# The down projection of a hybrid trunk: from a plain product to Strassen's seven, on one Trainium2 core

## The chip, the cores and the metric

The kernel runs on one core of one Trainium2 chip. The core has a matrix engine (PE, TensorE, with its weight loads listed as PEld), a vector engine (DVE, VectorE), a scalar engine (ACT, ScalarE), a general engine (POOL, GpSimd), and SyncE (SP), which here issues nearly all DMAs. Operands lie in SBUF (128 partitions), matmuls write PSUM. The metric is the device time of one execution in microseconds; less is better.

## The reference

One layer of a token mixer (an S5 state-space branch and an mLSTM branch) followed by a channel mixer, on 16 meta tokens and 2048 tokens of width 1024, in float32. The change is in the channel mixer:

```python
FFN_DIM = 2816

def channel_mixer(x, g_pre, g_post, w_gate, w_up, w_conv, b_conv, w_down):
    h = rmsnorm(x, g_pre)
    a = causal_dwconv(h @ w_gate, w_conv, b_conv)
    y = (jax.nn.gelu(a, approximate=True) * (h @ w_up)) @ w_down
    return x + rmsnorm(y, g_post)
```

The last product is the down projection: 2048 tokens x 2816 by 2816 x 1024. The result is normalised over its 1024 columns, scaled by `g_post` and added to x (in the kernel: to `h1_d`, the residual stream in DRAM).

## The kernel before

**Precision.** Every large product is made of three matmuls. An operand `a` is split into a high part (ScalarE copies `a` into the matmul type float32r) and a low part (VectorE subtracts the high part from `a`); `mm3` (lines 172 to 174) and `mm3x` (177 to 179) then add high x high, high x low and low x high into one PSUM tile. So each operand costs one ScalarE and one VectorE pass before TensorE may use it.

**The FFN stage.** `ffn_unit(p, m, ...)` handles block m (of NF = 22 blocks of 128 FFN channels) for token half p. Gate and up projections together are already one Strassen product: seven products of four depth blocks each, in the order 1, 6, 2, 7, 5, 4, 3, whose moving operands `op[n]` (sums of parts of the normalised input) stay in SBUF for the whole half, in pairs of tiles t4(0) to t4(11) and q4(0), q4(1). Each unit loads its weight blocks (`weights_first`, `weights_second`), forms the sums and splits them (`weight_op`, lines 1124 and 1125). For p = 0 a product runs in two pieces of 258 and 256 columns, for p = 1 in one of 512. After each product VectorE or ScalarE takes the PSUM tile into a running sum; then come the three-tap convolution (line 1254 on ScalarE, 1256 on VectorE), the GELU (1257), the product with the up projection (1261) and the store of the unit's y block to DRAM (`y_d`, line 1262, on SP's queue).

**Other work beside it.** In units 1 to 8 of p = 0 rows of the last token blocks are normalised (`norm_rows`, `norm_cols`); in units 10 to 17 `sums_piece` forms the sums that p = 1 needs as operands. In the last unit of p = 0, `turn` loads and splits four operands of p = 1 as their tiles come free. Staging tiles come from the pool `mk` (three places of about 1 MB).

**The down projection before.** It runs over two halves `nh` of 512 output columns. All 22 weight blocks of the half are loaded (four at a time through `mk`) and split (lines 1328 and 1329) into the tiles t4(0) to t4(10). Then for each of 16 tiles of 128 tokens the y blocks come back from DRAM in three chunks of 8, 8 and 6 (`ys`, line 1335), are split (1338, 1339) and serve as stationary operands of 22 x 3 matmuls of 512 columns into one PSUM tile. ScalarE forms the sum of squares (1345), VectorE multiplies by the gains. For `nh` = 0 the result stays in SBUF (`o0`); for `nh` = 1 the tile's row scale is computed (`rstd_of`, POOL at line 107), a row tile of `h1_d` is loaded, two multiply-adds (1358) make the output and two DMAs store it.

**What sets the order.** The tile framework keeps the program order of the code as a priority and orders each engine's instructions by a planned timeline; it adds all waits. On the chip each engine runs that order, one after the other, and each waits in place. Tiles of a pool take places as the tags are first used; a pool that is opened after another was closed lies where that one lay, and a new tile waits for the old tiles that it covers.

## Time and profile before

| | us |
|---|---|
| median of 3 runs | 2792.69 (2790.66 to 2794.34) |
| the profiled execution, its own time | 2792.36 |
| its span | 2790.6 |
| granted TensorE clock, mean | 0.998 |
| PE busy | 2759.1 |
| DVE busy | 1761.1 |
| ACT busy | 1054.7 |
| bytes moved by DMA | 395.47 MB, mean 142 GB/s |

The span is the time from the first to the last instruction of one profiled execution; times in a trace count from its start. A table by stretches gives, for each stretch of the span, the busy time of each engine with its instructions in brackets, then the granted clock (1.00 is full), the share of the 16 DMA engines that was busy, and GB/s. A row of a group gives line, engine, operation, output<-input, shape and count, then busy time in us and the mean of one in ns, then the idle time before it and what ended it. Matmuls are pipelined: the mean of one in such a row is longer than the distance to the next, so the rate is read from counts by time. The FFN stage lies between about 1430 and 2302 us, the down projection from 2287 to the end.

### The profile page before, as it was taken

To read this page: it belongs to the slowest core of one execution; us is meant where nothing else is said; L and a number is where in the kernel's file an instruction comes from. 1 tells how busy PE (TensorE), PEld (TensorE's weight loads), DVE (VectorE), ACT (ScalarE), POOL (GpSimd) and SP (SyncE) were. 2 spreads that over 40 slices of the span, in tenths; PEclk is the share of its full clock that TensorE was granted. 3 is DMA by queue.
4 is the path that set the end of the run, shared out by engine and by line. 5 is a ranking of instruction groups with operands and counts; after the bars stand their busy time and mean duration, and the time that the engine had idled before them with its cause. 6 is when DMAs were issued, how large, how long until landed. Compare 5 with 4: busy or idle time off the path is not lost.

```text
span 2790.6 us, 40815 instructions
## 1 busy us (share of the span) xinstructions
PE 2759.1 (99%) x15590; PEld 2484.9 (89%) x15590; DVE 1761.1 (63%) x3429; ACT 1054.7 (38%) x1979; POOL 136.8 (5%) x225
## 2 busy tenths in 40 slices
PE   8999999999999999999999999999999999999999
PEld 8999999999999987777799999998788788888887
DVE  4637799377555464676798887786776683224333
ACT  6102344233444444344354434453443352224221
POOL 1000000000000000000100000000000000000000
PEclk9999999999999999999999999999999999999999
DMA  9333443212454574667744462252222244335453
GB/s 309 106 79 131 158 147 121 71 69 72 145 159 144 167 212 121 223 196 250 265 157 138 159 234 87 73 176 85 80 80 81 79 145 149 99 90 165 157 166 128
DMA packets 323478, 395.47 MB, mean 142 GB/s; under 512 B 40321, under 2 KB 229142, under 8 KB 322642
## 3 DMA queue, kind: packets, MB, share of 16 engines
q1 hardware_dynamic: 323282, 392.86, 43.9%
q8 instruction: 122, 2.00, 0.3%
q14 instruction: 74, 0.61, 0.1%
HBM read 284.47 MB, written 108.31 MB: 141 GB/s over the span
## 4 chain that ended last, share of the span: by engine, by line
PE 82%; DMA 7%; DVE 6%; ACT 1%; issue 1%; POOL 1%; SPq 0%; DVEq 0%; POOLq 0%; ACTq 0%
PE mm L172 10%; PE mm L174 10%; PE mm L173 10%; PE ac L173 9%; PE ac L174 9%; PE ac L172 8%; PE ac L179 4%; PE ac L178 4%; PE ac L177 4%; PE mm L177 3%; PE mm L179 3%; PE mm L178 3%; DMA wu<-in_w_up_dram 2%; DMA gat<-gab_d 1%; DVE w L1125 1%
## 5 line engine op out<-in xcount | busy, mean ns | idle before, releaser
L174 PE MATMUL mm<-hTh,wl 128*128 128x410 f32 (+3 forms) x1216 | 428.0, 352 | 0.0
L172 PE MATMUL mm<-hTh,wh 128*128 128x410 f32 (+3 forms) x1216 | 427.6, 352 | 0.0
L173 PE MATMUL mm<-hTl,wh 128*128 128x410 f32 (+3 forms) x1216 | 427.4, 352 | 0.0
L1339 DVE TENSOR_TENSOR yhl<-ys,yhl 128x1024 fp32r<-128x1024 f32 (+1 forms) x96 | 109.1, 1137 | 291.9 <-ACT yhl L1338 291.9
L173 PE MATMUL ac<-t,yhl 128*128 128x512 f32 x704 | 278.5, 396 | 0.0
L174 PE MATMUL ac<-t,yhl 128*128 128x512 f32 x704 | 277.3, 394 | 0.0
L172 PE MATMUL ac<-t,yhl 128*128 128x512 f32 x704 | 276.6, 393 | 0.0
L177 PE MATMUL mm<-t,w 128*128 128x258 f32 (+2 forms) x792 | 253.7, 321 | 3.5 <-DVE u L1226 2.6
L178 PE MATMUL mm<-t,w 128*128 128x258 f32 (+2 forms) x792 | 253.5, 320 | 0.4 <-DVE t L1069 0.4
L177 PE MATMUL ac<-t,w 128*128 128x258 f32 (+2 forms) x792 | 253.2, 320 | 0.6 <-ACT u L1217 0.6
L179 PE MATMUL ac<-t,w 128*128 128x258 f32 (+2 forms) x792 | 253.1, 320 | 0.1
L179 PE MATMUL mm<-t,w 128*128 128x258 f32 (+2 forms) x792 | 252.5, 320 | 0.7 <-DVE w L1125 0.7
L178 PE MATMUL ac<-t,w 128*128 128x258 f32 (+2 forms) x792 | 253.1, 320 | 0.0
L173 PEld LDWEIGHTS mm<-hTl,wh 128*128 128x128 f32 x1216 | 228.7, 188 | 2.6
L174 PEld LDWEIGHTS mm<-hTh,wl 128*128 128x128 f32 x1216 | 228.8, 188 | 2.3
L172 PEld LDWEIGHTS mm<-hTh,wh 128*128 128x128 f32 x1216 | 228.7, 188 | 2.0
L1338 ACT ACTIVATE yhl<-ys 128x1024 fp32r<-128x1024 f32 (+1 forms) x96 | 95.0, 990 | 348.4 <-PE ac L173 345.9
L156 ACT ACTIVATE wh<-ws 128x1024 fp32r<-128x1024 f32 x104 | 109.9, 1059 | 237.8 <-PE mm L173 137.5
L1124 ACT ACTIVATE w<-s 128x512 fp32r<-128x512 f32 x176 | 109.3, 628 | 164.7 <-DVE s L1139 70.3
L177 PEld LDWEIGHTS mm<-t,w 128*128 128x128 f32 x792 | 149.7, 189 | 18.0 <-DVE u L1226 4.4
L172 PEld LDWEIGHTS ac<-t,yhl 128*128 128x128 f32 x704 | 132.4, 188 | 32.3
L177 PEld LDWEIGHTS ac<-t,w 128*128 128x128 f32 x792 | 149.2, 189 | 13.0 <-ACT u L1217 1.1
(453 smaller groups left out, 6074.1 us busy)
## 6 DMA issues: line engine op xcount, KB each, us to landing
ys<-y_d SPq DMA_DIRECT2D x64, 512.0 KB, 3.7
wg<-in_w_gate_dram SPq DMA_DIRECT2D x44, 512.0 KB, 3.6
wu<-in_w_up_dram SPq DMA_DIRECT2D x44, 512.0 KB, 4.3
gab_d<-ev SPq DMA_DIRECT2D x80, 205.0 KB, 2.4
ws<-in_w_m_dram SPq DMA_DIRECT2D x32, 512.0 KB, 3.8
ws<-in_w_ba_dram SPq DMA_DIRECT2D x32, 512.0 KB, 4.0
ws<-in_w_out_dram SPq DMA_DIRECT2D x32, 512.0 KB, 5.3
gat<-gab_d SPq DMA_DIRECT2D x48, 256.0 KB, 4.8
```

What stands on the lines that cost most here:

```text
L156: S.activation(wh, ws, AF.Copy, scale=scale)
L172: T.matmul(out=ps, lhsT=lh, rhs=rh, start=first, stop=False)
L173: T.matmul(out=ps, lhsT=lh, rhs=rl, start=False, stop=False)
L174: T.matmul(out=ps, lhsT=ll, rhs=rh, start=False, stop=last)
L177: T.matmul(out=ps, lhsT=lh, rhs=rh, start=first, stop=False, skip_group_check=True)
L178: T.matmul(out=ps, lhsT=lh, rhs=rl, start=False, stop=False, skip_group_check=True)
L179: T.matmul(out=ps, lhsT=ll, rhs=rh, start=False, stop=last, skip_group_check=True)
L1124: S.activation(t[:, 0], src, AF.Copy)
L1125: V.tensor_tensor(t[:, 1], src, t[:, 0].bitcast(F32), ALU.subtract)
L1338: S.activation(yh, ys, AF.Copy)
L1339: V.tensor_tensor(yl, ys, yh.bitcast(F32), ALU.subtract)
```

## The change

The down projection becomes one level of Strassen's algorithm (Winograd's form with seven products, the same order 1, 6, 2, 7, 5, 4, 3). Per half `nh` of 512 columns the weights are cut into two row halves (blocks 0 to 10 and 11 to 21) and two column halves of 256; tokens are taken in pairs of tiles, i and i + 4. A product is 11 depth blocks x 3 matmuls of 256 columns, and all 11 blocks of the seven weight operands of a half stay in SBUF: 8 blocks in the FFN's operand tiles (`wmain`), 3 in new tiles (`wrest`).

The sums are made ahead, during the FFN stage: `down_weight_sums` in units 1 to 4 and 14 to 21 of p = 0, `down_input_sums` in units 1 to 11 and 13 to 21 of p = 1 (tokens of the first and second half), each in three steps, load and then four VectorE sums and then four stores to DRAM (`wt_d`, `s_d`) that are issued on ScalarE's queue. Two pieces of input sums (`last_sums`) are made in the down stage itself. `sums_piece` moves to units 9 to 14. The y stores of the FFN go to ScalarE's queue and are issued in the unit after, behind its third product; so do the stores of the output. In the last unit of p = 1, `turn_down` loads and splits the eight-block parts of six operands. The pools of weights and staging tiles are then closed, and the pool `dn` takes their place.

In the down stage a stationary operand (1408 columns) is loaded in two half pieces through five places (`raw`) and split into one of two places (`st`); the split for the next product is issued ahead of a product's matmuls, the loads for two or three products on behind it. Results of the first column half go to DRAM (`yo_d`) and are read back for the output; before, they stayed in SBUF. The weights of the second half come piece by piece through the same five places during the last products of the first half.

The diff, cut to its core:

```diff
+    def down_weight_sums(nh, k):
+        kn = min(2, 11 - k)
+        t = mk_tile()[:, 0:kn * 1024].rearrange("p (k b n) -> p k b n", k=kn, b=4)
+        for h in range(2):
+            r0 = (k + 11 * h) * 128
+            P.dma_start(out=t[:, :, 2 * h:2 * h + 2].rearrange("p k b n -> p k (b n)"),
+                        in_=w_down[r0:r0 + kn * 128, nh * 512:(nh + 1) * 512].rearrange("(k p) n -> p k n", k=kn))
+        yield
+        b11, b12, b21, b22 = (t[:, :, b] for b in range(4))
+        V.tensor_tensor(b11, b12, b11, ALU.subtract)
...
+        yield
+        for b in range(4):
+            S.dma_start(out=wt_d[nh, b, :, k:k + kn, :], in_=t[:, :, b])
...
@@ ffn_unit
             prod(A, 2, False)
             S.activation(gp_[:, x0 + p0:x0 + p0 + pn], A, AF.Copy)
+            while late_y:
+                late_y.pop(0)()
...
-            P.dma_start(out=y_d[m, :, p * 1024 + o0:p * 1024 + o1], in_=c)
+            late_y.append(lambda o0=o0, o1=o1, c=c: S.dma_start(out=y_d[m, :, p * 1024 + o0:p * 1024 + o1], in_=c))
...
+    def turn_down():
+        for n in ORDER[:6]:
+            t = mk_tile()[:, 0:2048]
+            P.dma_start(out=t.rearrange("p (k n) -> p k n", k=8), in_=down_src(0, n, 0, 8))
+            places(n)
+            for h in range(2):
+                main_split(n, h, t[:, h * 1024:h * 1024 + 1024])
...
+    def raw_tile(n):
+        return dn.tile([128, 768], F32, tag="raw", name="raw", bufs=5)[:, 0:n]
...
+    def st_split(i):
...
+        st = dn.tile([128, 2, 1408], F32R, tag=f"st{turn_[0] % 2}", name="st")
+        for raw, c0, c1 in zip(raw_of.pop(i), (0, 768), (768, 1408)):
+            split(st[:, 0, c0:c1], st[:, 1, c0:c1], raw)
...
+        def prod(ps, n, first):
+            i = PR.index((nh, j, n))
+            st_split(i + 1)
+            w_splits()
+            turning = i < 7 or first_i <= i < last_i + 7
+            st_loads(i + 2 if turning else i + 3)
+            for f in before(i):
+                f()
+            st = st_of.pop(i)
+            for k in range(11):
+                mm3x(ps, st[:, 0, k], st[:, 1, k], moving(n, 0, k), moving(n, 1, k), first and k == 0, k == 10)
+            if n in (1, 3):
+                while later:
+                    later.pop(0)()
+
+        def done(row, col, src):
+            dst = o[row][:, col * 256:col * 256 + 256]
+            jk = pst("tp", [128, 256])
+            S.activation(jk, src, AF.Square, accum_out=sq4[tl[row]][:, nh * 2 + col:nh * 2 + col + 1])
+            V.tensor_tensor(dst, src, g4[:, col * 256:col * 256 + 256], ALU.mult)
...
+    def finish(t, o1):
+        sm = dn.tile([128, 1], F32, tag="sm", name="sm", bufs=2)
+        V.tensor_reduce(out=sm, in_=sq4[t], op=ALU.add, axis=mybir.AxisListType.X)
+        rs = rstd_of(Small(dn, "r", 2), sm, 128, 1, 1.0 / D)
+        y0 = dn.tile([128, 512], F32, tag="y0", name="y0")
+        P.dma_start(out=y0, in_=yo_d[t])
+        for hh, src in ((1, o1), (0, y0)):
+            cs_ = slice(hh * 512, hh * 512 + 512)
+            ht = dn.tile([128, 512], F32, tag="ht", name="ht")
+            P.dma_start(out=ht, in_=h1_d[NM + t * 128:NM + (t + 1) * 128, cs_])
+            V.scalar_tensor_tensor(src, src, rs, ht, ALU.mult, ALU.add)
+            later.append(lambda cs_=cs_, src=src: S.dma_start(out=out[t * 128:(t + 1) * 128, cs_], in_=src))
...
+    second = [lambda n=n, part=part: w_load(1, n, part) for n in ORDER for part in range(4)]
+    cut = [0, 2, 4, 6, 8, 10, 12, 14, 16, 19, 22, 25, 28, 28]
```

249 lines of the change are left out of this document (193 added, 56 removed).

## The prediction

> **What bounds the kernel now.** I read the page's busy shares first, then its chain of waits, then tables of busy time by stretch for the last stages.
>
> ```profile
> PE 2759.1 (99%) x15590; PEld 2484.9 (89%) x15590; DVE 1761.1 (63%) x3429; ACT 1054.7 (38%) x1979; POOL 136.8 (5%) x225
> PE 82%; DMA 7%; DVE 6%; ACT 1%; issue 1%; POOL 1%; SPq 0%; DVEq 0%; POOLq 0%; ACTq 0%
> ```
>
> TensorE is busy for 99% of the span and holds 82% of the chain, so time is saved only by taking matmul time away, and lost wherever something makes TensorE stand. The next fence has, by stretch (us, then busy time and count of PE, PEld, DVE, ACT, POOL, then clock, DMA share, GB/s), the down projection, two units of the FFN's first half, one of its second half, and the sums over 22 units of either half.
>
> ```profile
> 2330.00:2520.00 190.00, 190.00 (x820) 153.63 (x819) 49.34 (x50) 43.63 (x61) 0.00 (x0) 1.00 0.32 94
> 1697.60:1717.80 20.20, 20.20 (x171) 20.20 (x171) 15.18 (x30) 8.46 (x15) 0.19 (x1) 1.00 0.25 81
> 1859.20:1879.40 20.20, 19.42 (x95) 15.67 (x94) 19.91 (x32) 12.68 (x19) 5.75 (x2) 1.00 0.84 293
> 2016.80:2036.40 19.60, 19.60 (x86) 15.88 (x85) 13.27 (x22) 7.50 (x13) 0.49 (x1) 1.00 0.24 72
> sum 444.40, PE 441.99 PEld 436.74 DVE 364.76 ACT 201.63 POOL 22.01; mean PE 20.09 PEld 19.85 DVE 16.58 ACT 9.17 POOL 1.00
> sum 430.10, PE 428.48 PEld 345.53 DVE 307.82 ACT 181.11 POOL 25.01; mean PE 19.48 PEld 15.71 DVE 13.99 ACT 8.23 POOL 1.14
> ```
>
> Down, a matmul of 512 columns takes 190.00/820 = 0.2317 us. In the FFN's first half, where every product is cut into pieces of 258 and 256 columns, one takes 20.20/171 = 0.1181 us, at the full clock in both. Half the columns cost 0.51 of the time: that is the price the change needs.
>
> **The change, part by part: the matmuls.** Before: 2 halves x 16 token tiles x 22 x 3 = 2112 of 512 columns, 2112 x 0.2317 = 489.4 us. After: 2 halves x 8 pairs of tiles x 7 products x 11 x 3 = 3696 of 256 columns, 3696 x 0.1181 = 436.6 us; one product is 33 x 0.1181 = 3.90 us, a pair 27.3. The last matmul of before:
>
> ```profile
> 2783.34 0.39 PE L174 MATMUL ac<-t,yhl 128*128 128x512 f32 x1
> 2786.16 1.41 DVE L1358 SCALAR_TENSOR_TENSOR ht<-o,rs,ht 128x512 f32<-128x512 f32 x2 [0.73 <-POOL rs L107]
> ```
>
> It starts at 2783.34 and its slot ends at 2783.6. With no gaps, the FFN's matmuls stand for the time up to 2783.6 - 489.4 = 2294.2, and the new last matmul ends at 2294.2 + 436.6 = 2730.8: 52.8 us earlier. Everything below is what is given back.
>
> **Tail.** Before, the span (2790.6) ends 7.0 us after the last matmul. After, two token tiles end together, and each needs two gathers of h1 through one place and one load of a kept half through one place, in a chain: 2.5 us from the last products to a scale (2783.6 to 2786.16), then reloads one behind the other. A load of 256 KB is not in the trace; I bound its landing by the 256 KB store (2.2) and the 512 KB load (4.6):
>
> ```profile
> ht<-h_d SPq DMA_DIRECT2D x16, 512.0 KB, 4.6
> out_dram<-ht SPq DMA_DIRECT2D x32, 256.0 KB, 2.2
> ```
>
> The first tile's second reload lands some 2 us after the last matmul, its multiply-add 0.75, then two more reloads of 2.5 to 3 with 0.75 each, about 9.3; from the last multiply-add of before (2787.6) to the span's end were 3.0. So 12 (10 to 16), 5 more than before: 2742.8.
>
> **FFN stage, F.** Added: four 512-column sums in 12 units of the first half and 20 of the second, and 216 stores on ScalarE. DVE's price: back to back such an operation takes 0.60.
>
> ```profile
> 2287.08 2.50 DVE L1329 TENSOR_TENSOR t<-mk,t 128x512 fp32r<-128x512 f32 x4
> 2290.43 3.75 ACT L1328 ACTIVATE t<-mk 128x512 fp32r<-128x512 f32 x7
> L1262 SPq EVENT_SEMAPHORE  x80: 17/17/11152, 1441.7 to 2307.0; - x80
> L1262 SPq DMA_DIRECT2D y_d<-cc x88: 319/327/981, 1435.2 to 2307.2; - x88
> ```
>
> Four are 2.4 us: DVE goes from 15.2 to 17.6 of 20.2 us in a plain unit, from 13.3 to 15.7 of 19.6 in the second half. Both hide behind TensorE. They don't hide in the stretch 1859 to 1879, the turn between the halves, where DVE is at 19.91 of 20.20 and a weight piece now falls too: +2.4. ScalarE issues 6 DMAs of 0.33 in a unit, 2 us on 8.5 of 20.2: hidden; its next instruction waits behind each, but the y stores are issued in the next unit, after its third product, when their data is long there. In the early units, which also normalise rows, the room is smaller: that is in the upper end. Against it, SyncE no longer waits up to 11.2 us for y with weight loads queued behind. TensorE's whole idle time in the 44 units is 2.4 + 1.6 = 4.0 us, so that is the most it can give. F = +3 (-4 to +8).
>
> The Trainium skill (DMA: Bandwidth & Descriptors, section Rules for kernel authors) says that spreading DMAs over issuing engines brings no bandwidth and only saves issue time. By it the moved stores are worth 0 rather than up to 4 us; the row speaks of a wait, which the rule leaves out, and I count 1 of the 4.
>
> **The turn into the down projection, T1.** In the last unit the six weight places are split while its own operands come free. Around the same point of before:
>
> ```profile
> 2270.00:2287.00 17.00, 17.00 (x74) 13.59 (x73) 16.73 (x27) 12.45 (x22) 2.60 (x2) 1.00 0.48 154
> 2287.00:2302.00 15.00, 15.00 (x67) 12.15 (x66) 14.62 (x24) 10.15 (x19) 0.13 (x1) 1.00 0.87 281
> L172 PE MATMUL ac<-t,yhl 128*128 128x512 f32 x13 | 5.1, 392 | 0.0
> L177 PE MATMUL mm<-t,w 128*128 128x512 f32 x4 | 1.6, 396 | 0.0
> ```
>
> DVE is full there (31.4 of 32 us), and the last unit was late; TensorE stayed busy because it slipped in 3 x 13 down matmuls (x13 on each of three lines between 2287 and 2302), 9.0 us of filler. The new order has none: the first product needs its place of stationary halves, and the new pool starts where the closed ones lay, so by the tiles' sizes that place (15.0 to 26.0 KB) reaches into the first weight staging tile (from 24.0 KB), and the rest weights lie on the third. Both wait for the turn's last splits. DVE in the last unit: 5 sums of products 3.0, two halves of the convolution 3.8, one piece's sums 2.4, and 12 low parts of 1024 columns at 1.13, 13.6; together 22.8 against 84 x 0.2317 = 19.5 of TensorE. Then the first product's first low part, 0.87: 23.7; with the last 1 MB load through three places I put the start at 26 to 27. T1 = 7, from 3 (DVE's sum alone) to 12 (the 9.0 of filler, 2.4 for the first splits, and hops). The Trainium skill (TensorE: Matmul & The Clock Gate, section Loop structure matters more than you think) adds that an idle gap of more than about 3 us halves the clock for a while, which I would estimate at 2 us more; no gap of that size with such a drop stands in the rows I quote.
>
> **Steady products.** Each product's 1408 columns are split in pieces of 768 and 640. Rows of before, with 640 by a line between them:
>
> ```profile
> L1339 DVE TENSOR_TENSOR yhl<-ys,yhl 128x1024 fp32r<-128x1024 f32 x64 | 78.4, 1226 | 227.7 <-ACT yhl L1338 227.7
> L1338 ACT ACTIVATE yhl<-ys 128x1024 fp32r<-128x1024 f32 x64 | 67.9, 1061 | 232.6 <-PE ac L173 230.1 <-DMA ys<-y_d 2.5
> L1339 DVE TENSOR_TENSOR yhl<-ys,yhl 128x768 fp32r<-128x768 f32 x32 | 30.7, 959 | 64.2 <-ACT yhl L1338 64.2
> L1338 ACT ACTIVATE yhl<-ys 128x768 fp32r<-128x768 f32 x32 | 27.1, 848 | 115.8 <-PE ac L173 115.8
> L1226 DVE TENSOR_TENSOR u<-mm,u 128x256 f32<-128x256 f32 x17 | 7.2, 422 | 2.0 <-PE mm L179 2.0
> ```
>
> ScalarE 0.85 + 0.74, DVE 0.96 + 0.83 (0.87 + 0.73 back to back). DVE per pair: 7 x 1.60 + 9 evacuations at 0.33 = 14.2 of 27.3. A split starts when the product before last frees one of two places; with a square and sum ahead of it, its first low part is ready 0.56 + 0.85 + 0.96 and three hops of 0.1, 2.7 us on, 1.2 before TensorE asks. In the first column half nothing is late: S0 = 1 (0 to 6, the rest weights and two pieces of sums in the first 17 products).
>
> **The turn between column halves, T2.** 28 weight pieces go through the same five places over 13 products. DVE: 13 x 1.60 + 7 x (3 x 0.87 + 0.60) + 5.5 of evacuations = 48.8 of 13 x 3.90 = 50.7. At 96% the cover is gone whenever a piece lands late: T2 = 5 (0 to 14, when 1.1 us of each product shows).
>
> **The second column half, S1.** A pair adds 4 multiply-adds and small ones, 3.6 us of DVE (17.8 of 27.3), so no engine is the bound; but three of four h1 reloads start only when the one before is consumed, and DVE, in order, sits at the next. Landing differs by 4.6 - 2.2 = 2.4; less the 1.2 of margin, one such stall in a pair is 1.2 x 8 = 10 us. None if other work stands ahead: 0; three in every pair: 30. S1 = 10.
>
> **Sum.** 2742.8 + 3 + 7 + 1 + 5 + 10 = 2768.8 of span. The execution profiled took 2792.36 for a span of 2790.6, 1.8 more, and agrees with the median 2792.69. So 2770.6; I say 2771, 0.8% faster.
>
> **Rivals.** *Everything hides* (12%): low ends but for 3 at the turn, 2742.8 + 3 + 1.8 = 2748. *Given back* (10%): the terms near their upper ends, 47 to 52 us together, 2792, no change. *The transfers become the bound, slower* (16%): after the turn a pair loads 14 pieces, 7 x 721 KB = 5.05 MB, and in the second half 2.6 MB of kept halves, h1 and output, 7.7 MB in 27.3 us = 281 GB/s. Such rates are in the rows of 2287 to 2302, share 0.87, and there landings are longer than in the calm page rows:
>
> ```profile
> ys<-y_d SPq DMA_DIRECT2D x3, 512.0 KB, 6.6
> ys<-y_d SPq DMA_DIRECT2D x64, 512.0 KB, 3.7
> mk<-h_d SPq DMA_DIRECT2D x7, 1024.0 KB, 7.8
> ```
>
> Five places serve two pieces a product, so a place may be taken for 2.5 x 3.90 = 9.75 us: landing plus about 3 until it is split. Above a landing of 6.75 TensorE runs at the places' pace. At 7.8 a product takes 10.8/2.5 = 4.32, 0.42 more; over all 112 products, 47, and in place of S1, 2771 - 10 + 47 = 2808. The sign turns at about 32 us: a landing of 7.5 in both halves, or of 8.2 in the second alone. For it: 281 GB/s. Against: 6.6 is still under 6.75, for larger pieces. *A fixed cost per matmul* (1%): if halving the columns saved little, e.g. 0.75 of the time, 3696 x 0.75 x 0.2317 = 642 us and about 2977. The Trainium skill (TensorE: Matmul & The Clock Gate, section Back-to-back issue gap) has about 81 ns at 128 columns and 131 at 512, by a line 98 at 256, 0.75; the 0.51 of the rows decides against it. *Forecast* (61%): own range 2752 to 2786.
>
> **How the numbers follow.** A measurement of this kernel tells about 0.2%, 5.6 us, from no change. Faster holds the forecast and the first rival, 0.73; same 0.10; slower 0.17. The range starts at 2747, with the first rival, and on the upper side takes in half of the transfer rival, to 2802.
>
> **What would show it.** Right: matmuls of 256 columns 0.118 apart, a gap of 3 to 12 us at the start of the down stage, gaps of about a microsecond in the second half ended by DVE's low parts behind an h1 load, DMA share above 0.8 there. Wrong: gaps ended by the half pieces' DMA in every product, FFN units longer than 20.2 and 19.6, or 256 columns costing over 0.125.

## The result, and the profile after

The changed kernel takes 2831.66 us (median of 4 runs, 2829.53 to 2834.76) against 2793.52 for the kernel before (2790.66 to 2796.53): a ratio of 1.0137, interval 1.012 to 1.0155. It is slower by 1.4%; the forecast was 2771. The profiled execution has a span of 2828.3 us and took 2830.12.

Busy shares and chain of waits from the page of the changed kernel:

```profile
PE 2733.2 (97%) x17174; PEld 2538.4 (90%) x17174; DVE 1973.3 (70%) x3811; ACT 1152.4 (41%) x2193; POOL 135.9 (5%) x225
PE 64%; DMA 17%; DVE 13%; issue 2%; ACT 2%; POOL 1%; SPq 0%; DVEq 0%; ACTq 0%; POOLq 0%
DMA packets 404287, 516.65 MB, mean 183 GB/s; under 512 B 46993, under 2 KB 278054, under 8 KB 402914
```

TensorE has less to do, as meant, but holds 64% of the chain where it held 82%; DMA went from 7 to 17% and VectorE from 6 to 13%. Before, 395 MB were moved, now 517. A stretch table shows where (columns as in the prediction: busy time and count of PE, PEld, DVE, ACT, POOL, then clock, DMA share, GB/s). First the kernel before, in three stretches of the FFN stage:

```profile
1640.00:1700.00 60.00, 60.00 (x503) 60.00 (x503) 46.53 (x92) 25.63 (x46) 1.14 (x4) 1.00 0.39 129
1862.00:1950.00 88.00, 87.22 (x375) 70.06 (x374) 65.42 (x104) 36.90 (x60) 8.44 (x5) 1.00 0.37 124
2000.00:2080.00 80.00, 80.00 (x346) 64.86 (x345) 55.15 (x88) 31.86 (x52) 5.58 (x4) 1.00 0.25 79
```

The same stretches after, and behind them, in the down projection, a part of pair 0, the steady part, the turn between the column halves, and the second half:

```profile
1640.00:1700.00 60.00, 56.27 (x465) 55.64 (x464) 54.93 (x111) 22.62 (x42) 3.23 (x3) 1.00 0.96 323
1862.00:1950.00 88.00, 79.31 (x353) 63.17 (x352) 80.62 (x129) 35.22 (x55) 8.83 (x4) 0.98 0.93 301
2000.00:2080.00 80.00, 80.00 (x346) 64.77 (x345) 56.89 (x90) 33.45 (x54) 4.07 (x4) 1.00 0.26 86
2342.00:2365.00 23.00, 20.55 (x165) 19.59 (x164) 17.70 (x25) 14.63 (x24) 0.00 (x0) 1.00 1.00 334
2400.00:2520.00 120.00, 120.00 (x1018) 120.00 (x1017) 68.58 (x102) 53.38 (x100) 0.00 (x0) 1.00 0.70 212
2530.00:2620.00 90.00, 77.16 (x568) 72.68 (x567) 62.58 (x91) 52.08 (x87) 2.34 (x2) 0.94 0.86 277
2640.00:2740.00 100.00, 96.05 (x785) 94.56 (x784) 60.40 (x103) 41.49 (x78) 5.79 (x8) 0.98 0.84 264
```

Read the DMA share beside the matmul counts. Where it is 0.26 to 0.70, TensorE has no gap, and the steady down projection runs at 120.00/1018 = 0.1179 us a matmul, the price that was forecast. Where it is 0.84 to 1.00, matmuls are missing. (The share alone is no proof: in the row of 2287 to 2302 of the prediction the kernel before has 0.87 and no gap, with other matmuls to slip in.) And the FFN's sums are not spread: between 2000 and 2080, four units in which the code writes four input pieces, there is no more traffic than before (86 against 79 GB/s). They stand earlier. DMA issues of the changed kernel between 1862 and 1950 (count, KB each, median us to landing), then between 2000 and 2080:

```profile
mk<-y_d SPq DMA_DIRECT2D x20, 512.0 KB, 5.8
s_d<-mk ACTq DMA_DIRECT2D x33, 256.0 KB, 4.8
wu<-in_w_up_dram SPq DMA_DIRECT2D x4, 512.0 KB, 6.7
```

```profile
wu<-in_w_up_dram SPq DMA_DIRECT2D x4, 512.0 KB, 4.1
```

Twenty loads are ten pieces in four and a half units: the planned order issued each piece as soon as its data was there. An up weight then lands after 6.7 us, not 4.1. Pieces of the chain of waits in that stretch:

```profile
1899.41 7.79 DMA s_d<-mk
...
1907.63 6.73 DMA mk<-y_d
...
1923.10 8.78 DMA wu<-in_w_up_dram
```

A staging place waits for a store's landing, a piece for its load, and the units for weights. The start of the down projection, TensorE's instructions one by one:

```profile
2330.26 0.58 PE L180 MATMUL ac<-t,st 128*128 128x256 f32 x1 [10.60 <-ACT st L1384]
...
2332.07 0.41 PE L182 MATMUL ac<-t,st 128*128 128x256 f32 x1
2332.28 0.41 PE L180 MATMUL ac<-t,st 128*128 128x256 f32 x1
...
2333.91 0.28 PE L182 MATMUL ac<-t,st 128*128 128x256 f32 x1
```

and its stretch behind the gap:

```profile
2330.20:2334.00 3.80, 3.54 (x15) 3.25 (x16) 3.76 (x5) 2.84 (x5) 0.00 (x0) 0.53 0.69 229
```

10.6 us of gap, ended by ScalarE's split of the first stationary operand. The first 14 matmuls behind it take 3.65 us, most of them 0.21 apart, at a granted clock of 0.53; then they are 0.12 apart.

To compare runs I use times between starts of matmuls: a *unit* is 168 matmuls in the FFN's first half and 84 in its second, a *pair* of the down projection 231 (27.3 us without a gap). *Stage* runs from the first FFN matmul to the last, *gap* from there to the first down matmul. Before, by the prediction's 2294.2 for the end without the filler of down matmuls, the stage is 2294.2 - 1403.8 = 890.4; counted by its own starts, 2301.7 - 1403.8 less 39 filler matmuls of 0.2317, it is 888.9. The two differ by 1.5 us, so comparisons with the stage before are no finer than that.

| | forecast, given back | measured | lost |
|---|---|---|---|
| FFN stage | 3 | ends at 2319.3, not 2294.2 | 25 |
| gap | 7 | 2330.3 - 2319.3 | 11 |
| pairs 0 to 7 | 1 | 34.9 (pair 0), 191.3 (1 to 7) | 8 |
| pair 8, the turn | 5 | 47.3 | 20 |
| pairs 9 to 15 | 10 | 209.2, of 191.1 | 18 |
| tail | 12 | 2828.3 - 2813.0 | 15 |

The FFN stage by itself is 28 us longer (30 by its own starts); the stages before it, which the change doesn't touch, ended 3 us sooner in this execution (they end between 1400 and 1408 us in the runs below). In all 97 us are lost where 38 were forecast.

### The profile page after: what moved, and what is told of

It is laid out like the page before. It is cut to its first block, busy times and chain, and to the rows that moved or that the text cites. A ratio compares the mean times of both kernels' runs of the same rounds, so it can differ in the third digit from the quotient of the medians.

```text
span 2828.3 us, 45651 instructions
## 1 busy us (share of the span) xinstructions
PE 2733.2 (97%) x17174; PEld 2538.4 (90%) x17174; DVE 1973.3 (70%) x3811; ACT 1152.4 (41%) x2193; POOL 135.9 (5%) x225
## 4 chain that ended last, share of the span: by engine, by line
PE 64%; DMA 17%; DVE 13%; issue 2%; ACT 2%; POOL 1%; SPq 0%; DVEq 0%; ACTq 0%; POOLq 0%
PE mm L175 9%; PE mm L177 9%; PE mm L176 9%; PE ac L182 4%; PE ac L180 4%; PE ac L181 4%; DMA wu<-in_w_up_dram 4%; PE mm L180 3%; PE mm L181 3%; PE mm L182 3%; PE ac L176 3%; PE ac L177 3%; PE ac L175 3%; DVE w L1165 2%; DMA ht<-h_d 2%
## 5 line engine op out<-in xcount | busy, mean ns | idle before, releaser
L180 PE MATMUL ac<-t,w 128*128 128x256 f32 (+2 forms) x792 | 255.2, 323 | 11.9 <-ACT w L1164 6.6
L182 PE MATMUL ac<-t,w 128*128 128x256 f32 (+2 forms) x792 | 254.2, 322 | 4.9 <-DVE w L1165 4.7
L181 PE MATMUL ac<-t,w 128*128 128x256 f32 (+2 forms) x792 | 254.4, 322 | 0.0
L1384 ACT ACTIVATE st<-raw 128x768 fp32r<-128x768 f32 x224 | 166.5, 785 | 168.7 <-PE ac L182 45.3
L1385 DVE TENSOR_TENSOR st<-raw,st 128x768 fp32r<-128x768 f32 x224 | 190.9, 887 | 54.1 <-ACT st L1384 54.1
L180 PEld LDWEIGHTS ac<-t,w 128*128 128x128 f32 x792 | 150.2, 190 | 26.5 <-ACT w L1164 8.6
L180 PEld LDWEIGHTS mm<-t,w 128*128 128x128 f32 x792 | 150.0, 190 | 23.6 <-DVE u L1270 6.3
L182 PEld LDWEIGHTS ac<-t,w 128*128 128x128 f32 x792 | 150.5, 190 | 18.7 <-DVE w L1165 7.1
L182 PEld LDWEIGHTS mm<-t,w 128*128 128x128 f32 x792 | 149.7, 189 | 12.6 <-DVE w L1165 0.9
L181 PEld LDWEIGHTS ac<-t,w 128*128 128x128 f32 x792 | 150.7, 190 | 11.4
L181 PEld LDWEIGHTS mm<-t,w 128*128 128x128 f32 x792 | 149.9, 189 | 12.2 <-DVE t L1074 0.9
```

The source lines that it names most:

```text
L180: T.matmul(out=ps, lhsT=lh, rhs=rh, start=first, stop=False, skip_group_check=True)
L181: T.matmul(out=ps, lhsT=lh, rhs=rl, start=False, stop=False, skip_group_check=True)
L182: T.matmul(out=ps, lhsT=ll, rhs=rh, start=False, stop=last, skip_group_check=True)
L1384: S.activation(hi, raw, AF.Copy)
L1385: V.tensor_tensor(lo, raw, hi.bitcast(F32), ALU.subtract)
```

## The experiments

| run | time | before, same chip | stage | gap | pair 0 | pairs 1-3 | pair 8 | pairs 10-15 |
|---|---|---|---|---|---|---|---|---|
| changed kernel | 2831.7 | 2793.5 | 918.7 | 11.0 | 34.9 | 81.8 | 47.3 | 177.7 |
| e1_y_on_sp | 2836.8 | 2797.7 | 917.2 | 15.4 | 35.4 | 82.4 | 45.0 | 174.9 |
| e2_four_places | 2851.8 | 2797.7 | 919.7 | 11.0 | 39.5 | 86.2 | 51.5 | 178.5 |
| e3_two_h1 | 2827.9 | 2797.7 | 920.9 | 11.0 | 35.1 | 82.3 | 45.5 | 170.3 |
| e4_lent | 2821.8 | 2797.7 | 916.9 | 10.9 | 35.2 | 81.9 | 38.2 | 172.0 |
| e5_insum_late | 2839.3 | 2789.1 | 931.0 | 7.2 | 34.0 | 86.3 | 45.8 | 174.0 |
| e6_wsum_moved | 2839.0 | 2789.1 | 935.3 | 9.3 | 34.1 | 82.9 | 45.3 | 170.9 |
| e7_no_adds | 2835.7 | 2789.1 | 929.7 | 8.0 | 35.1 | 81.8 | 45.7 | 173.7 |
| c1_all | 2823.4 | 2789.1 | 928.3 | 9.4 | 34.1 | 84.5 | 37.9 | 169.8 |
| e8_sums_pool | 2842.0 | 2794.3 | 928.9 | 11.9 | 36.0 | 83.0 | 46.6 | 174.3 |
| e9_weights_pool | 2840.8 | 2794.3 | 924.0 | 10.2 | 34.4 | 81.8 | 46.1 | 178.2 |
| e10_no_sums | 2817.1 | 2794.3 | 906.5 | 9.4 | 31.1 | 81.8 | 46.9 | 177.4 |
| e11_pinned | 2823.5 | 2793.7 | 913.3 | 11.1 | 34.8 | 81.8 | 46.3 | 174.5 |
| c2_all | 2795.9 | 2793.7 | 901.7 | 7.0 | 37.1 | 84.8 | 37.6 | 169.9 |
| c3_halo | 2792.6 | 2798.1 | 894.4 | 7.9 | 30.7 | 88.9 | 38.8 | 171.1 |
| c3_pool | 2796.5 | 2798.1 | 897.9 | 8.1 | 31.3 | 89.4 | 37.1 | 171.2 |
| c4_all | 2796.5 | 2794.5 | 895.2 | 4.0 | 33.3 | 95.9 | 37.6 | 171.7 |
| c5_all | 2788.3 | 2797.2 | 894.0 | 1.9 | 33.3 | 88.2 | 37.4 | 171.1 |
| e12_no_h1 | 2813.3 | 2798.0 | 921.0 | 11.3 | 34.9 | 81.9 | 45.8 | 166.5 |

The runs are single but for the first row, c4_all and c5_all. e2, e3, e4 and e12 leave the FFN as it is and have stages of 916.9 to 921.0; kernels with the changed kernel's down projection have pairs 10 to 15 at 170.9 to 178.2. Smaller differences than these say nothing.

**e1_y_on_sp**, y stores back on SP:

```diff
-            late_y.append(lambda o0=o0, o1=o1, c=c: S.dma_start(out=y_d[m, :, p * 1024 + o0:p * 1024 + o1], in_=c))
+            P.dma_start(out=y_d[m, :, p * 1024 + o0:p * 1024 + o1], in_=c)
```

> One part of the change undone: the stores of the gated result y go back to SyncE's queue, issued at the end of their own unit; all else is as in the changed kernel. Theory (the stage of the feed-forward products lost 25 us, and the part of it at units 16 to 19 of the second half, 7.5 us over 19.5 a unit, comes from a y load of an input-sum piece that waits on SyncE for a y store which ScalarE's queue issues a unit later, with the next gate weights queued behind it): these four units fall back to 19.5 to 20.5 us each, 4 to 7 us less, and nothing else changes by more than 2 us; the span falls from 2828 to 2821 to 2825. Rival (the wait only moves: the y store on SyncE then waits itself for the end of the gating and holds the next weights): these units stay above 21 us, others become longer, and the span is 2826 to 2836.

The stage is within the scatter; units 16 to 19 take 19.5, 20.4, 21.1 and 23.5 us, but unit 14 now 23.1, and the gap grew by 4. That looks like the rival, a wait that moved, but e3_two_h1 and e12_no_h1 have 23.6 and 23.7 at unit 14 with the y stores on ScalarE's queue: units 14 to 19 together take 126 to 128 us in all these runs, and in the changed kernel. So neither story is shown; where the y stores are issued is worth nothing that these runs resolve.

**e2_four_places** and **e4_lent** turn the number of places each way; e4_lent also cuts the main parts smaller (256 KB in place of up to 384):

```diff
-        return dn.tile([128, 768], F32, tag="raw", name="raw", bufs=5)[:, 0:n]
+        return dn.tile([128, 768], F32, tag="raw", name="raw", bufs=4)[:, 0:n]
```

> One size changed: four places of 384 KB in place of five, through which every operand piece of the down projection is loaded. Theory (at the turn between the column halves, 20 us lost, and in pairs 9 to 15, 18 us lost, the pace is that of the places: freed by a split, filled by a transfer of 4 to 7.5 us): with a place less, the turn, 47.3 us with five places, takes 50 to 58 us, pairs 9 to 15 gain 10 to 40 us together, and the span rises to 2840 to 2890; pairs 2 to 7 of the first half, 27.3 us each, stay within 1 us. Rival (the bound at the turn is the mean rate of the DMA engines, or the order of VectorE's work in the second half): the places' number matters little, the turn stays within 2 us, the pairs 9 to 15 within 4 us together, and the span is 2826 to 2834.

```diff
 def w_load(nh, n, part):
+        if nh:
+            k0, k1 = ((0, 2), (2, 4), (4, 6), (6, 8), (8, 11))[part]
...
+        if nh and part < 4:
+            lend[0] += 1
+            tag = LEND[lend[0] % len(LEND)]
+            raw = dn.tile([128, 512], F32, tag=tag, name="lent", bufs=LB[tag])
```

> The main parts of the second column half's weight operands no longer go through the five places: they are loaded in parts of 256 KB through three places of the output work (first-half reload, residual reload, late sums) that stand idle at the turn between the halves. Bytes, splits and products are the same. Theory (the turn lost 20 us to the pace of five places): the turn's pair, 47.3 us, falls to 31 to 40 us, and the span to 2813 to 2822. Rival (the DMA engines' rate bounds the turn: they show a busy share of 0.82 to 0.91 there and 260 to 311 GB/s): the pair stays at 44 us or more and the loss moves into pairs 7 and 9; the span is 2825 to 2835.

The stretch of the turn with four places, and then with the weights on lent places:

```profile
2530.00:2620.00 90.00, 73.93 (x535) 69.28 (x534) 58.07 (x81) 50.11 (x82) 0.00 (x0) 0.93 0.79 247
```

```profile
2530.00:2620.00 90.00, 82.49 (x646) 79.99 (x646) 66.41 (x104) 53.45 (x97) 1.10 (x2) 0.96 0.87 295
```

Places hold transfers open: 247, 277 and 295 GB/s with four, five and eight of them, pair 8 at 51.5, 47.3 and 38.2 us; of the 9 us that the lent places win there, pair 9 takes 3 back. That bears out the places at the turn, and a second limit behind them: 14 products ask for 14 x 0.72 + 7 x 1.44 = 20.2 MB in 54.6 us, 370 GB/s, and no stretch of 60 us in these tables shows more than 323 in the changed kernel. In pairs 10 to 15 a place less changes nothing (178.5, where 10 to 40 us were expected), so there the places are not the bound. Neither are they in steady pairs: 3 to 6 stay at 27.3 with four.

**e3_two_h1** and **e12_no_h1** take the reload of the residual, in one place, apart:

```diff
-            ht = dn.tile([128, 512], F32, tag="ht", name="ht")
+            ht = dn.tile([128, 512], F32, tag="ht", name="ht", bufs=2)
```

> One size changed: two places in place of one for the reload of the first residual in the second column half of the down projection (the place used only by the late input sums is given up for it). Theory (pairs 9 to 15 lose 18 us because VectorE, in order, stands at a multiply-add until the one place's reload has landed, and the splits of the next operands wait behind it): pairs 9 to 15, 209.7 us together against 191.5 without a loss, fall to 194 to 202 us, and the span falls by 8 to 16 us to 2812 to 2820. Rival (they lose it to the places of the operand loads, whose pieces land late beside stores, reloads and first-half reloads): they stay at 206 us or more, and the span is 2825 to 2832.

```diff
-            P.dma_start(out=ht, in_=h1_d[NM + t * 128:NM + (t + 1) * 128, cs_])
-            V.scalar_tensor_tensor(src, src, rs, ht, ALU.mult, ALU.add)
+            V.scalar_tensor_tensor(src, src, rs, g4_of[0], ALU.mult, ALU.add)
```

> Made from the changed kernel. Left out: the reload of the first residual in the second column half; the last multiply-add adds the gains in its place, so the output is another. Four loads of 256 KB a pair fall away and with them the wait of VectorE for each; the reload of the first column half stays. Theory (pairs 10 to 15 lose what they lose because VectorE, in order, stands at a reload while the next operand's pieces wait to be split; two places in place of one took 177.7 us to 170.3): they fall to 164 to 167 us, 27.3 to 27.8 each. Rival (the transfers bound them, 7.7 MB a pair, of which the residual is 1.0): they keep half of the loss or more, 171 or above. The turn between the halves, 47.3 us, stays within 2 us by both.

VectorE's waits in the second column half (us in total, times, longest) of the changed kernel, and of e3_two_h1:

```profile
DVE y L1571 <- DMA ht<-h_d: 25.2, 13, 3.4
DVE o L1571 <- DMA ht<-h_d: 17.1, 7, 3.3
```

```profile
DVE y L1571 <- DMA y<-yo_d: 19.7, 7, 3.2
...
DVE o L1571 <- DMA ht<-h_d: 5.2, 4, 2.0
```

Two places take 37 us of waits for the residual away and let 20 us of waits for the kept half appear, which is late next; pairs 10 to 15 at 170.3 lie at the edge of the scatter, half of what the theory wanted; the tail falls from 15.3 to 10.8. Without the reload the stretch reads:

```profile
2640.00:2740.00 100.00, 99.23 (x836) 98.61 (x835) 66.49 (x113) 42.85 (x80) 4.43 (x8) 1.00 0.78 249
```

836 matmuls in place of 785, pairs 10 to 15 at 166.5, 27.75 each, inside the theory's 164 to 167, 11 us under the changed kernel's own run and 4 under the shortest with that part unchanged. The rate hardly fell (264 to 249). That speaks for the wait in VectorE's order and against the transfers' rate; the edit takes the wait and 1.0 MB a pair away together.

**e5_insum_late**, **e6_wsum_moved** (W0 is 10, 13 and 14 to 21, W1 is 0 and 12), **e7_no_adds** and **c1_all** looked for the FFN's loss in single pieces; the diffs are those of the first three, c1_all joins e3 to e6 (with W1 as 12 and 13):

```diff
-        i = m - 1 if m < 12 else m - 13
+        i = m - 1 if m < 12 else m - 14
```

```diff
-        w_piece = wsum.pop(0) if 1 <= m < 5 or 14 <= m < 22 else None
+        w_piece = wsum.pop(0) if m in W0 else None
...
+        if m in W1:
+            w_piece = wsum.pop(0)
+            piece_turn(down_weight_sums(w_piece // 6, w_piece % 6 * 2))
```

```diff
-        V.tensor_tensor(b11, b12, b11, ALU.subtract)
...
-        V.tensor_tensor(a22, a21, a22, ALU.add)
...
```

> One thing moved: in the second half of the feed-forward stage each late input-sum piece is issued one unit later, so that the y block it loads has been stored by ScalarE's queue before; the piece that no longer fits is made in the down projection with two other late ones (three instead of two). Theory (units 16 to 19 of that half, 21.1, 21.3, 21.1 and 23.5 us in the changed kernel against 19.5 for a plain unit, lose 9 us because SyncE stands at the y load of this piece with the next gate weights queued behind it): these units fall to 19.5 to 20 us each, 6 to 9 us less in sum; the units 0 to 3 and the first half's units stay as they are within 2 us; the down projection loses 0 to 3 us for the third late piece. Rival (they lose it to the DMA engines or to VectorE, whenever the piece comes): the same loss shows one unit later, within 2 us in sum.

> One thing moved: the weight-sum pieces of units 1 to 4 of the first half of the feed-forward stage are made in units 10 and 13 of that half and in units 0 and 12 of the second, where no other helper's work stands. Theory (units 1 to 4 lose 10.9 us against the kernel before, 26.5, 27.0, 21.8 and 21.8 us against 23.8, 20.3, 20.8 and 21.0, because the pieces' loads wait on SyncE for staging places and hold the gate weights behind them): units 1 to 4 fall to 84 to 88 us in sum, from 97; the units that take the pieces over stay within 1 us each. Rival (what disturbs these units is work that the kernel before had there too, late norms and residual reloads, and the sums' DMA only adds to it): they fall by less than 5 us or the loss goes with the pieces to their new units.

> Left out: the four sums and differences on VectorE of every weight-sum and input-sum piece in the feed-forward stage (their loads and stores stay; the two input-sum pieces made in the down projection keep theirs), so the down projection works on operands that are not the sums. Theory (the adds, 2.4 us of VectorE a unit, lie beside the products, and what the stage lost is DMA waits on SyncE's queue): the stage from the first feed-forward product to the last, 918.7 us, changes by less than 4 us, and the span is 2823 to 2832. Rival (VectorE's order is what the products wait for): the stage falls by 10 to 25 us, and the span is 2803 to 2819.

> Four edits together: the second column half's weight operands in parts of 256 KB through idle output places (three: one for the first-half reload, two for the residual reload), two places for the residual reload, input sums a unit later, weight sums out of units 1 to 4. Theory (each loss has the cause named for it, and they add up): the feed-forward stage 918.7 us falls to 898 to 908, the turn's pair 47.3 us to 36 to 40, pairs 9 to 15 from 209.2 us to 198 to 205; the span 2790 to 2805. Rival (they share one limit, the DMA engines, and a gain at one place is lost at the next): the span 2806 to 2820.

In the FFN none did what its theory said. Late input sums: units 16 to 19 are 20.9, 21.1, 25.6 and 20.2, the last 27.2, the stage 12 us longer. Moved weight sums: units 1 to 4 fall to 86.1, as they should, but units 11 and 13 rise to 25.2 and 23.3, and units 1 to 4 of the second half to 95.5 from 85.2; stage 935.3. Without the adds the stage is 11 us longer, not 10 to 25 shorter: VectorE's price was not the matter, but the theory's 4 us does not hold either. Each edit made another planned order. c1_all has the down projection's gains that it expected (pair 8 at 37.9, pairs 9 to 15 at 201.6) and loses 10 us in the FFN; its span, 2821.6, lies above even its rival's.

**e8_sums_pool** and **e9_weights_pool** ask whether it is the queue:

```diff
-            P.dma_start(out=t[:, h * 1024:h * 1024 + 1024], in_=y_d[m + 11 * h, :, p * 1024:(p + 1) * 1024])
+            G.dma_start(out=t[:, h * 1024:h * 1024 + 1024], in_=y_d[m + 11 * h, :, p * 1024:(p + 1) * 1024])
```

```diff
-        P.dma_start(out=wg, in_=w_gate[m])
+        (G if m else P).dma_start(out=wg, in_=w_gate[m])
```

> One thing moved: the loads of the weight-sum and input-sum pieces in the feed-forward stage are issued on GpSimd's queue in place of SyncE's; everything else, the three staging places too, is as in the changed kernel. Theory (the stage's 25 us are lost because SyncE, in the order that was planned ahead, stands at a piece's load until a staging place or a y block has landed, 77 us of it in the second half for the places and 72 for the y blocks, with gate and up weights queued behind): nothing is queued behind these loads now, and the stage from its first product to its last, 918.7 us in the changed kernel and about 894 in the kernel before, falls to 895 to 907; the span is 2803 to 2818. Rival (the added traffic itself makes the weights land late, whichever queue issues it): the stage stays at 913 or more and the span at 2822 or more.

> One thing moved, the other way about: the gate and up weights of every unit but the first are issued on GpSimd's queue, and the sum pieces stay on SyncE's. Theory (the weights are late because they are queued behind the pieces' loads): the stage falls from 918.7 us to 895 to 907, as with the pieces moved. Rival (the weights land late for the traffic): 913 or more. A second rival (GpSimd's queue is itself in order, and its small copies for the convolution wait behind a weight load that waits for its place): the stage grows to 920 or more, with idle time of VectorE that GpSimd's copies end.

With the sums' loads on GpSimd's queue units 16 to 19 of the second half are plain again (19.6, 19.6, 19.9, 19.5), some 8 us less, so there the queue had its part. But units 20 and 21 give 6 of them back (45.5 us in place of 39.2), units 2 and 3 take 26.9 and 26.5, and the stage is 10 us longer: with no load in front of them the weights are late still. e9_weights_pool, 924.0, lies 3 us above the scatter; between 1862 and 1950 its up weights, on GpSimd's queue, land after 8.5 us. Its second rival's sign, VectorE idle until a GpSimd copy, isn't in the trace. The theory of the queue falls as the main cause; the traffic is left.

**e10_no_sums**:

```diff
-        piece_turn(None if w_piece is None else down_weight_sums(w_piece // 6, w_piece % 6 * 2))
...
-        piece_turn(down_input_sums(int(m > 12), i) if m not in (0, 12) else None)
...
-        if n in (1, 2, 3):
+        if n:
```

> Left out: all sums, in the feed-forward stage and in the down projection, loads, additions and stores; the products that need them take unsummed blocks from the same tensors, the same bytes in shorter runs. Theory (everything the feed-forward stage lost comes with the sum pieces, and the y stores on ScalarE's queue cost nothing by themselves): the stage falls from 918.7 us to 890 to 898, the time of the kernel before. Rival (the moved y stores, the moved operand sums of the second half and the handover between the halves lose part of it): 902 to 912. For the down projection only this is expected: without the two late sums pair 0 stays above 33 us, because its loss is the loads of the last weight parts beside those of the stationary halves.

Its stretches in the second half of the FFN, and a group of its matmuls between 2000 and 2280 (busy us, mean ns, then idle time and what ended it):

```profile
1862.00:1950.00 88.00, 87.63 (x394) 71.23 (x393) 66.39 (x106) 39.29 (x62) 8.43 (x5) 1.00 0.40 134
2000.00:2080.00 80.00, 78.14 (x331) 61.77 (x331) 53.15 (x86) 30.10 (x50) 8.59 (x4) 1.00 0.25 79
L182 PE MATMUL ac<-t,w 128*128 128x512 f32 x165 | 64.3, 403 | 6.6 <-DVE w L1165 6.6
```

The burst is gone and its matmuls are back. But the stage is 906.5, not 898, inside the rival's 902 to 912: units 6 to 20 of the second half now take 20.3 to 21.0 in place of 19.5, at a DMA share of 0.25. About half of it stands in the third row: in each unit a low part of a weight comes late from VectorE. It isn't the moved y stores as such, which the rival names: the changed kernel has them too, and its units 5 to 15 stand at 19.5 to 19.7. That the planned order has a price of its own is the explanation left; which step of it costs is open. (ScalarE's convolution waits 14.3 us in the second half for GpSimd's two-column copy, against 5.0 before and 4.4 in the changed kernel; no run takes that apart here.) Pair 0 falls from 34.9 to 31.1 without the late sums, so half of its loss goes with them; the theory had it above 33.

**e11_pinned** changes order alone:

```diff
+        last_w[0] = P.dma_start(out=wu, in_=w_up[m])
...
-            next(new)
+            with tc.issue_after(last_w[0].ins):   # SP's order only, no wait
+                next(new)
```

> Order only: the loads of each weight-sum and input-sum piece are queued on SyncE behind the up weights of the unit in which the code writes the piece; no wait is added, nothing else is edited. In the changed kernel the planned order draws the pieces together: between 1862 and 1950 us, four and a half units, stand 20 loads of y blocks, ten pieces written for units 1 to 10, at a DMA share of 0.85 to 1.02, and none between 2000 and 2080. Theory (the feed-forward stage loses its time in these bursts, because the weights of the next unit land late beside them, and not for the pieces as such or for the queue they are on): spread out one to a unit, units 0 to 3 of the second half fall from 88.9 us to 78 to 81, units 9 to 13 of the first half from 106 to 101 to 103, and the stage from 918.7 us to 898 to 908; units 1 to 4 of the first half, where the pieces are spread less, keep most of their loss. Span 2806 to 2820. Rival (a piece in a unit costs wherever it stands): the loss spreads with the pieces, units 4 to 11 of the second half rise above 20 us, and the stage stays at 914 or more.

Its stretches, and its y loads between 1862 and 1950:

```profile
1640.00:1700.00 60.00, 60.00 (x502) 59.80 (x500) 50.23 (x100) 25.66 (x47) 0.95 (x3) 1.00 0.37 122
1862.00:1950.00 88.00, 85.42 (x389) 69.33 (x388) 74.90 (x120) 40.67 (x63) 13.92 (x5) 1.00 0.58 188
2000.00:2080.00 80.00, 79.00 (x339) 63.43 (x338) 64.10 (x104) 30.27 (x51) 2.57 (x4) 1.00 0.59 186
mk<-y_d SPq DMA_DIRECT2D x8, 512.0 KB, 6.9
```

Eight loads where there were twenty, the same share in both stretches, and in the two bursts the matmuls are back: units 0 to 3 80.1 us (88.9, and 88.6 to 89.7 in the runs that leave the FFN as it is), units 9 to 13 101.0 (105.4), as the theory said. The stage, 913.3, misses its 908 and nearly reaches the rival's 914: five of the units 5 to 13 of the second half now lose 0.6 to 2.0 us, units 14 to 21 stand at 19.5 to 23.6, and units 1 and 2 of the first half keep 10. Bursts are shown as the cause where the bursts stood; of the 13 us won there 8 come back in other units. c3_halo, below, shows that this is no price of the pieces as such.

**c2_all, c3_halo, c3_pool, c4_all, c5_all** add the causes up. c2_all joins e3, e4 and e11, takes the weight pieces out of units 1 to 4 and the input pieces a unit later, with none in the last unit and four late ones. The others stand on the one before them (c4_all on c3_halo, c5_all on c4_all without its place for late sums); the diffs are what is new in c3_halo, c3_pool, c4_all and c5_all:

```diff
+            with tc.issue_after(last_w[0].ins):
+                P.dma_start(out=t, in_=y_d[m + 11 * h, :, 1024 + 512 * c:1536 + 512 * c])
...
-            G.tensor_copy(gp_[:, 2:4], halo[:, m])
+            V.tensor_copy(gp_[:, 2:4], halo[:, m])
```

```diff
+                main_split(n, h, t[:, h * 1024:h * 1024 + 1024], G if n in (5, 4) else V)
```

```diff
+        a12 = raw_tile(512)
...
+            if n == FIRST_AT:
+                first_st()
```

```diff
+        elif 6 <= i < 24:
+            for g, q in ((late_store, i - 8), (late_sums, i - 7), (late_load, i - 6)):
+                if 0 <= q < 16:
+                    f.append(lambda g=g, q=q: g(q))
```

> Together: pieces kept in their units as in the run with order only, no weight-sum pieces in units 1 to 4 of the first half (they go to units 10 and 13 and to 12 and 13 of the second), input sums one unit later with none in the last unit (four late ones in the down projection), and in the down projection the second half's weights through idle output places and two places for the residual reload. Theory: the stage 893 to 903 us, the gap at the start of the down projection 4 to 9 in place of 10.6 (no piece's store stands ahead of the last operands' loads), pair 8 at 36 to 40, pairs 9 to 15 at 198 to 207; span 2780 to 2798. Rival (whatever is spread or moved comes back at the next place that is full): span 2805 or more.

> The last combination with two edits more. The loads of the four late input sums, which the planned order drew forward into pair 0 of the down projection, are queued behind the operand loads of the product in which the code writes them; and the two-column copy that starts each convolution of the second half moves from GpSimd to VectorE, since ScalarE's convolution stood 2.9 and 3.9 us for it at the two worst units (15 and 21). Theory: pairs 0 and 1, 37.1 and 29.5 us, fall to 32 to 35 and 27.3 to 28; units 15 and 21, 23.8 and 23.6 us, fall by 2 to 4 each; span 2776 to 2788. Rival (pair 0 is bound by its own operand loads, and the copy's wait is covered): pair 0 stays above 36, the units above 23, and the span is 2790 to 2798.

> As the run before it, and the low parts of the last two operands that are split in the last feed-forward unit (four pieces of 1024 columns) go from VectorE to GpSimd. Theory (the start of the down projection waits for VectorE, which has 22.8 us of work in a unit of 19.5): the gap before the first down product, 6.7 us, falls to 2 to 5 and the last unit by 1 to 3; span 2 to 6 us less than the run before it. Rival (GpSimd is slower at it than the products come, or holds VectorE back): the first products of pair 0 wait for GpSimd, and the span is the same or up to 10 us more.

> As the combination with VectorE's halo copy, with two edits more. The late input sums no longer use a place of the output rows (the fourth tile goes through one of the five operand places, and their stores are issued a product later): in the run before, 3.0 us of gap at 2379 us was ended by ScalarE's first write into an output row, whose place a late sum's store still held. And the first stationary operand of the down projection is loaded through a staging place and split into the two tiles of the last feed-forward operand, ahead of the last unit's convolution: its split stood on ScalarE behind that convolution and the y store, from 2302 to 2307, while its operand had landed. Theory: pairs 1 to 3, 29.2, 31.3 and 28.4 us, fall to 28 or less each; the gap before the first down product, 7.5 us, falls to 1 to 3, of which pair 0 (30.7) gives 1 to 3 back; span 2779 to 2787, and the time 0.2 to 0.6% under the kernel before. Rival (pairs 0 to 3 are bound by the DMA engines, which work at a share of 1.0 there, and what is won at the gap is lost in pair 0): the span is 2788 to 2793.

> As the run before it, but the four late input sums are cut into 16 quarters (128 tokens of one block pair: two loads and one store of 128 KB each way, four sums of 128 columns), one to a product from product 6 to 21, in the idle output places alone; no place of output rows or of operands is taken. Theory (pairs 1 to 3 lost 17 us in the run before because a late sum held an operand place until its store had landed): pairs 1 to 3 fall to 27.3 to 28.5 each, the start of the down projection stays as it was (37 us from the last feed-forward product to pair 1), the span is 2776 to 2785 and the time 0.3 to 0.7% under the kernel before. Rival (the pairs lose it to the added traffic at a DMA share near 1.0, however it is cut): pairs 1 to 3 stay at 29 or more on the mean and the time is within 0.2% of the kernel before.

c2_all wins 17 us of the stage, 4 of the gap, 10 of pair 8, and is level with the kernel before; all its theory's ranges hold. What GpSimd's copy did ahead of its unit 15 (23.8 us), POOL's group of 22 copies and the one row, then ScalarE's row:

```profile
L1244 POOL COPY gp<-halo 128x2 f32<-128x2 f32 x22 | 28.1, 1278 | 392.6 <-DVE cc L1302 317.2 <-ACT w L1164 75.5
```

```profile
2157.07 2.90 POOL L1244 COPY gp<-halo 128x2 f32<-128x2 f32 x1 [19.95 <-DVE cc L1302]
```

```profile
2160.01 0.82 ACT L1300 ACTIVATE cc<-gp,cbf,cwf 128x512 f32<-128x512 f32 x1 [1.45 <-POOL gp L1244]
```

and the same copy on VectorE in c3_halo (shortest, median and longest, ns):

```profile
L1244 DVE COPY gp<-halo x22: 159/162/169, 1882.9 to 2289.4; 128x2 f32<-128x2 f32 x22
```

With it units 1 to 20 of the second half are all at 19.5 to 19.6, and the stage is 894.4, 4 us over the kernel before. Its stretch over most of the second half:

```profile
1900.00:2280.00 380.00, 380.00 (x1636) 307.59 (x1635) 318.10 (x529) 158.83 (x257) 0.00 (x0) 1.00 0.59 192
```

No gap in 380 us, with the pieces' loads, sums and stores beside the products: held to their units, they hide. One edit was the copy, but the order changed with it, so how much is the copy's own is open: the kernel before has the same copy on GpSimd, 1.16 us on the mean, in units as plain as these, and in c3_halo ScalarE still waits 12.4 us for it on VectorE without a unit losing. Unit 21 stays at 24.2, where 2 to 4 us less were expected. Pair 0 falls to 30.7 once the late sums are kept out of it, but pairs 1 to 3 rise from 84.8 to 88.9: the traffic came after it. Low parts on GpSimd (c3_pool) help nothing: the last unit 27.4, the gap 8.1. The gap, in ScalarE's rows of c3_halo:

```profile
2302.55 0.81 ACT L1300 ACTIVATE cc<-gp,cbf,cwf 128x512 f32<-128x512 f32 x1 [3.28 <-DVE gp L1282]
2304.97 0.63 ACT L1303 ACTIVATE cc<-cc 128x512 f32<-128x512 f32 x1 [1.61 <-DVE cc L1302]
2306.36 0.33 ACTq L1308 DMA_DIRECT2D y_d<-cc  x1
2306.78 1.47 ACT L1388 ACTIVATE st<-raw 128x768 fp32r<-128x768 f32 x2 [1.18 <-DVE cc L1307]
```

The first split stands behind the last unit's convolution, GELU and y store, which themselves wait for VectorE. c4_all puts it ahead: the gap falls by 3.9 to 4.0, and pair 0 takes 2.6 of that back; but its late sums in an operand place make pairs 1 to 3 95.9 (a place of output rows held by a late sum, which they were to spare, was the smaller matter), and it times at 1.0005 of the kernel before (0.9996 to 1.0014). c5_all's quarters bring these pairs to 88.2, not to the 82 to 85.5 expected (29.4 a pair is the rival's range, that the traffic costs however it is cut), and the gap to 1.9:

```profile
2300.11 0.39 PE L180 MATMUL ac<-t,q 128*128 128x256 f32 x1 [1.55 <-ACT q L1388]
```

c5_all beats both kernels: 2788.33 us (7 runs, 2785.83 to 2791.88) against 2797.22 for the kernel before on the same chip, 0.9974 (0.9963 to 0.9985), a little less than the 0.3% expected. Of the 52.8 us that the products save it keeps 9.

## Why the prediction was wrong

Three terms of the sum left their ranges: F and T2 by far, S0 by 2 us. They priced the time of the engines and no bytes, and F took the order of the code for the order of the chip.

**The matmuls** were right: 0.1179 us against 0.1181, pairs without a gap 27.3.

**F, forecast 3 (-4 to 8), measured 25.** This step failed, and by most. It reads "four 512-column sums in 12 units of the first half and 20 of the second": it put the pieces where the code writes them and priced VectorE's and ScalarE's time. VectorE's part wasn't the loss: without the adds the stage is no shorter (e7_no_adds). The step never priced the 2.1 MB that each piece loads and stores, and it didn't ask where the planned order would put them. By its own rows a plain unit of the second half moves 72 GB/s; a piece in each gives 72 + 2.1/19.6 us, some 180, and c3_halo has 192 with no gap. Ten pieces in 88 us gave 301. By units, against the kernel before, the loss stands in units 0 to 3 of the second half (11 us) and 9 to 13 of the first (4), the bursts; in units 16 to 19 of the second (8); and in units 1 to 4 of the first (11), where the prediction saw less room and put it into the upper end: e6_wsum_moved, with the weight pieces out of them, has these at 86.1 again, the time of the kernel before. That the bursts cost what stood in them is shown by e11_pinned, and that pieces held to their units in the second half hide, by c3_halo. That the planned order costs something of its own without any piece is seen in e10_no_sums; that it is what the other edits ran into is only argued.

The Trainium skill (DMA: Bandwidth & Descriptors, section Rules for kernel authors) says that spreading DMAs over issuing engines brings no bandwidth. The runs agree: with the y stores, the sums' loads or the weights issued on another queue the stage was 917.2 us in e1_y_on_sp, 928.9 in e8_sums_pool and 924.0 in e9_weights_pool, against 918.7.

**T1, forecast 7 (3 to 12), measured 11.** In its range. Named was VectorE's work and a place that is free late; c4_all and c5_all show ScalarE's order ahead of the first split, in which VectorE's lateness stands too. Of the 3.9 and 6.0 us that they win there against c3_halo, 2.6 are lost again in pair 0, where the changed kernel's row shows a DMA share of 1.00.

The Trainium skill (TensorE: Matmul & The Clock Gate, section Loop structure matters more than you think) said that a gap of this size halves the clock for a while. It did: the first 14 matmuls behind the gap take 3.65 us in place of 14 x 0.118 = 1.65, so 2.0 us, with one wait of 0.2 us for VectorE among them; the estimate was 2.

**S0, forecast 1 (0 to 6), measured 8, all but 0.4 in pair 0.** It named "the rest weights and two pieces of sums" and gave them no bytes: in pair 0 operands, rest weights and the last weight operand are 5.05 + 5 x 0.39 + 1.05 = 8.1 MB, 295 GB/s, and the planned order drew the late sums' loads into it too. Without the sums 3.8 of the 7.6 us are left (e10_no_sums).

**T2, forecast 5 (0 to 14), measured 20.** This step failed too. It compared VectorE's 48.8 us with 50.7, allowed for a piece that lands late, and put no bytes to it. My rival's row had the sum that was missing: at its 281 GB/s the turn's 20.2 MB need 72 us, 17 more than 54.6. Measured are 277 GB/s and, pairs 7 and 8 together, 20.3 us. That the figures meet is in part luck: 281 is no ceiling, for with the lent places pairs 7 and 8 take 66.2 us for the same bytes, 305 GB/s. The mechanism of the rival, transfers that land too late for five places, is what e2_four_places and e4_lent bear out; its place was wrong: it wasn't the steady pairs, where 212 GB/s and even four places suffice, but the two turns of the down projection, and with them the FFN's bursts, where transfers meet that the prediction had apart.

**S1, forecast 10 (0 to 30), measured 18.** Mechanism right, a size off: pairs 10 to 15 lose 13.9, 2.3 a pair instead of 1.2. Without the residual's reload 2.7 are left (e12_no_h1), so it has 11 of them by the changed kernel's own run and at least 4 by the scatter. Pair 9 loses 4.2 as the turn's end.

**Tail, forecast 12 (10 to 16), measured 15.3.** VectorE's last rows show the chain of reloads as described, each up to about a microsecond longer than counted:

```profile
2815.89 0.75 DVE L1571 SCALAR_TENSOR_TENSOR y<-y,rs,ht 128x512 f32<-128x512 f32 x1 [1.10 <-DMA ht<-h_d]
...
2819.96 0.75 DVE L1571 SCALAR_TENSOR_TENSOR o<-o,rs,ht 128x512 f32<-128x512 f32 x1 [3.26 <-DMA ht<-h_d]
2824.63 0.75 DVE L1571 SCALAR_TENSOR_TENSOR y<-y,rs,ht 128x512 f32<-128x512 f32 x1 [3.92 <-DMA ht<-h_d]
```

The prediction says that a load of 256 KB is not in the trace. That is a misreading: earlier stages of the kernel before have many, as

```profile
ot<-o_d SPq DMA_DIRECT2D x16, 256.0 KB, 4.5
```

so the 2.5 to 3 us counted for a reload was low.

What the prediction named as a sign of its own failure came true in part: FFN units longer than 20.2 and 19.6. Gaps ended by the half pieces in every product did not come.

## What to carry to other kernels

When a change adds transfers, divide bytes by time for each stage and each turn between stages, not only for the steady part, and compare with the rates that the trace has reached; here the turns, in which the loads of two stages meet, lost most for their length. Work that is "spread over the units" is spread only if something holds it there: look in the trace where a planned order has put it, and pin it if it bunches. And price a removed matmul against what stands ready behind it: 53 us of TensorE were bought with 121 MB of DMA, and only after the order was mended at each of these places were 9 of them left.
